# Three blocks on one core: first mixers regrouped, VectorE's head steps chained in TensorE's order, query's gate products moved behind the inverse's first level, odd mixer's end in steps

## The chip, the cores and the metric

The kernel runs on one NeuronCore of a Trainium2 chip. Its time is device microseconds of one launch. Three runs of the kernel before took 1113.0, 1119.35 and 1120.01 us (median 1119.35). A profiled execution of the same program gives the trace.

## The reference, cut to what matters

512 tokens of width 1024 in float32 go through three residual blocks.

```python
# block 1: two mixers beside each other, then a gated MLP
proj = rms_norm(x) @ w_in             # q k v gate a b of 4 delta heads, q k v gate of 4 retention heads
qkv  = silu(causal_dwconv(q, k, v))   # 4 taps
q, k = l2norm(q) * d**-0.5, l2norm(k)
beta, g = sigmoid(b), -exp(a_log) * softplus(a + dt_bias)
m    = strict_lower(k k^T * beta * decay(g));  t_mat = inv(eye + m)
# chunk by chunk: u = t_mat v' - w S;  o = q_dec S + (q k^T * decay) u;  S = S*cd + k_dec^T u
h    = x + concat(rms(o_gdn) * norm_w * silu(gate), rms(o_ret) * silu(gate)) @ w_out
h    = h + (silu(g) * u) @ w_down     # g, u: 3-tap convolutions of rms_norm(h) @ w_up
x    = rms_norm(h)
# block 2 (even mixer): window attention and multi-scale pooling, gated, @ ab_w_out
# block 3 (odd mixer)
a, b, gate = split(rms_norm(x) @ c_w_in)
conv = causal_dwconv(a * sigmoid(b), dw_w) + dw_b       # 31 taps, channel by channel
y    = silu(layer_norm(conv)) * silu(gate)
out  = x + rms_norm(y @ c_w_out)
```

## The kernel before, in words

Activations lie transposed: 8 tiles of 128 channels x 512 tokens. Every large matrix product is done in three passes (`mm3`, lines 320 to 323): operand and weight are each split into a rounded part "hi" (a ScalarE copy to fp32r) and a remainder "lo" (a subtraction on VectorE or GpSimd), and hi*hi, hi*lo and lo*hi are accumulated in PSUM. One unit of 128 output channels is 8 x 3 = 24 matmuls of 512 columns. Weights come through SyncE's DMA queue in a fixed order: `fetch` issues one, `unpack` splits it, `prefetch` does both while buffers are free, `take` hands the next one out. While `lazy` is set, `prefetch` only issues a load and splits it in its next call.

**Block 1's mixers** (lines 505 to 999). `side_steps` runs the projection units in the order of `P1_ORDER`; the first call does three units together and with them the 8 columns of a and b: per input tile k two narrow matmuls of the split input with the 16 columns `wab` (line 357). `first_norm` makes the rms factor `rbc`, `do_ab` then turns a and b into the decay exponents `g` and what hangs on them. The eight heads are Python generators (`gdn_head`, `ret_head`, `finish_head`) that give up control at each `yield from need(n, lat, cost)`: the main loop at line 988 resumes one when a clock, kept from estimated TensorE costs, has passed its `lat`, else it emits one more step of a projection unit. So TensorE's and SyncE's order is the traced order (`manual_schedule`, `P1_ENG`), head work mixed into projection work; ScalarE, VectorE and GpSimd are put in order by the framework's scheduler.
`gdn_head`: squares and their sums give the norms of q and k (line 667 sums q's squares with 4 matmuls of one column), `decays` and `decays_exp` make exp(g_i - g_j), then k k^T and k q^T (lines 695 to 698), the inverse by 32x32 tiles in four levels (`tiles`, line 723), two block steps and the scan over four chunks.

**Block 3** (lines 1325 to 1555). `P7_ORDER` is an order written by hand: a = two projection units and the gated product of tile m (`glu_tile`), t, u, v = a copy of the tile shifted four ways (`stack_tile`), c = the convolution (`conv_tile`), s = its statistics, g = a gate unit, x = transposes of the residual, l = `norm_stats`, b = `spread` of its two results, n = `norm_tile`. Of the 31 taps TensorE does 4 per group (`PE_TAPS` groups, line 1402), ScalarE and GpSimd 3 (`N_POOL`), VectorE the rest, two of them (`P7_LEAD`) into an SBUF tile and the others into the group's PSUM bank. Up to l, PE, SP and DVE are in traced order; from l on only PE and SP. The output product follows: tokens 0 to 255 first (lines 1594 to 1603), whose k-th step needs tile k of `Y` from `norm_tile` and the k-th weight.

Of the kernel before, what the change touches and what calls it, by code (L numbers as in the profile page):

```python
# [20 lines left out]
C = 128  # L21
# [15 lines left out]
L_A0 = 9.0  # L37
L_AB = 13.0
L_PRE = 4.6
L_NORM = 15  # L40
L_M = 5.2
# [23 lines left out]
PE_TAPS = (4, 4, 4, 4, 4, 4, 4, 4)  # L65
# [4 lines left out]
P7_ORDER = 'a0 a1 t0 g0 u0 a2 v1 c0 a3 v2 c1 s0 a4 v3 c2 s1 a5 v4 c3 s2 a6 v5 c4 s3 a7 v6 c5 s4 g1 v7 c6 s5 g2 c7 g3 s6 x0 g4 x1 s7 g5 x2 l0 g6 b0 n0 n1 n2 n3 n4 n5 g7 n6 n7 x3'  # L70
# [83 lines left out]
def build(tc, xT, par, cst, rope, w_ab, w_in, w_rv, w_out, w_up, w_down, a_w, ab_w, c_w, co_w, post1, poolw, out, dbg=None):  # L154
# [192 lines left out]
    def side_steps(ws, X, sl=slice(0, T), ab=None):  # L347


        ps = [pu() for _ in ws]  # L350
        if ab is not None:
            pab = pu()
        for k in range(KD):
            x = X[k][0][:, sl], X[k][1][:, sl]
            if ab is not None:
                for i in range(2):
                    pe.matmul(pab[0:16], lhsT=ab[:, 16 * k:16 * k + 16], rhs=x[i], start=k + i == 0, stop=k == KD - 1 and i == 1)
            for w, p in zip(ws, ps):
                mm3(p[:, sl], wsl(w, k), x, k == 0, k == KD - 1)
            if k % 4 == 3:  # L360
# [185 lines left out]
    fr(*xin)  # L546
# [6 lines left out]
    def first_norm():  # L553
        yield from need(1, L_N1)
        rstd.append(small(NCH, "rstd", 1))
        by_chunk(rstd[0], rsqrt_rows(rbc, ssum))

    Y, O, gate, G = [None] * 8, [None] * 8, [None] * 8, {}

    def do_ab(p):  # L560

        ab = al()
        TT(ab[0:16], p[0:16, :], rbc[0:16, :], MUL)
        yield from need(1, L_A0)
        pt = pm()
        for c in range(NCH):
            pe.transpose(pt[:, c * 16:(c + 1) * 16], ab[0:16, ch(c)], ident[0:16, 0:16])
        fr(ab)
        pt4 = pt[:, 0:64].rearrange("p (c e) -> p c e", c=4)
        pv = sp.tile([128, 4, 8], F32, name="pv", bufs=1)  # L570
        dve.tensor_copy(out=pv, in_=pt4[:, :, 0:8])
        TT(pv, pv, pt4[:, :, 8:16], ADD)
        pm.fr(pt)
        s = lambda n: sp.tile([128, 4, 4], F32, tag=n, name=n, bufs=1)
        xa, nx, ex, beta, ea, g = s("xa"), s("nx"), s("ex"), s("beta"), s("ea"), s("g")
        TT(xa, pv[:, :, 0:4], bc4(pc("dtb", 0, 4)), ADD)
        TS(nx, xa, -1.0, MUL)
        TT(nx, nx, xa, MAX)
# [3 lines left out]
        A(ea[:, 0, :], pc("alog", 0, 4), AF.Exp)  # L582
        STT(g, xa, -1.0, bc4(ea[:, 0, :]), MUL, MUL)
        A(beta, pv[:, :, 4:8], AF.Exp, scale=-1.0)
        TS(beta, beta, 1.0, ADD)
        dve.reciprocal(out=beta, in_=beta)
        g2 = g.rearrange("p c h -> p (c h)")
        yield from need(1, L_AB, 0.4)
# [19 lines left out]
    def decays_exp(gm):  # L608
# [11 lines left out]
    def gdn_pre(p, h, which):  # L620
# [4 lines left out]
        A(acc, acc, AF.Silu)  # L625
# [34 lines left out]
    def gdn_head(h, qT, kT, vT):  # L660
        gm, sq = decays(h), al()
        A(sq, qT, AF.Square)
        yield from need(3, L_PRE)
        Ec, Es = decays_exp(gm)
        pss = pm()
        for c in range(NCH):
            pe.matmul(pss[:, c:c + 1], lhsT=sq[:, ch(c)], rhs=ones[:, 0:1], start=True, stop=True)
# [26 lines left out]
        pkk, pkq = pm(), pm()  # L694
        for c in range(NCH):
            pe.matmul(pkk[:, ch(c)], lhsT=kT[:, ch(c)], rhs=kT[:, ch(c)], start=True, stop=True)
        for c in range(NCH):
            pe.matmul(pkq[:, ch(c)], lhsT=kT[:, ch(c)], rhs=qT[:, ch(c)], start=True, stop=True)
        for c in range(NCH):
            STT(Mt[:, ch(c)], pkk[:, ch(c)], f[:, c:c + 1], Es[:, ch(c)], MUL, MUL)  # L700
        for c in range(NCH):
            STT(At[:, ch(c)], pkq[:, ch(c)], f[:, c:c + 1], Ec[:, ch(c)], MUL, MUL)
        pm.fr(pk, pkk, pkq)
        fr(Ec, Es)
# [21 lines left out]
        cost = 2.2  # L726
# [977 lines left out]
```

## Time and profile before

| | us |
|---|---|
| runs | 1113.0, 1119.35, 1120.01 |
| profiled execution, its own time | 1112.05 |
| span of its instructions | 1110.1 |

The page gives busy time per engine, the granted TensorE clock and the chain of work that ended last; the trace answers questions on stretches, waits and single instructions. A matmul's busy time reaches past the start of the next one, since they are pipelined, so the cost of one is read here from start to start. A plain float32 product stands in the trace as two matmul records.

### The profile page before, as it was taken

What the parts mean: (1) busy time and instruction counts of PE and PEld (TensorE: products, weight loads), DVE (VectorE), ACT (ScalarE), POOL (GpSimd) and SP (SyncE); (2) the same over time, 40 slices, a digit from 0 to 9 for tenths busy, and PEclk for the clock granted to TensorE, in tenths of its full rate; (3) what the DMA queues carried; (4) which work ended last, traced back from release to release, by engine and by line L of the source; (5) the groups of instructions that cost most, each with busy time, mean ns of one, the idle gap of its engine ahead of it and who ended that gap; (6) DMA issues with size and microseconds to landing.
All of it is one profiled execution on the core that took longest, in us unless ns stands there. A gap on an engine that the chain in (4) does not pass through costs nothing.

```text
span 1110.1 us, 17768 instructions
## 1 busy us (share of the span) xinstructions
PE 1086.1 (98%) x6882; PEld 875.2 (79%) x6882; DVE 755.6 (68%) x1555; ACT 523.2 (47%) x1052; POOL 225.0 (20%) x208
## 2 busy tenths in 40 slices
PE   8989999999999999999999999999999999999997
PEld 5777787888888888888888888766899996666776
DVE  7969567577567876767653244679856858669774
ACT  6774353226444544444353255365445565454351
POOL 0562231101020000000000024000000016988350
PEclk9989999999999999999999999999999999999989
DMA  8331112113323323333333332211223322221112
GB/s 289 112 96 43 57 58 77 58 48 124 95 78 103 105 95 95 96 100 105 98 93 93 100 106 85 89 39 58 76 77 107 122 58 77 76 77 38 39 39 76
DMA packets 28948, 96.02 MB, mean 86 GB/s; under 512 B 3552, under 2 KB 3808, under 8 KB 28864
## 3 DMA queue, kind: packets, MB, share of 16 engines
q1 hardware_dynamic: 27936, 91.87, 26.0%
q0 software_dynamic: 928, 3.02, 0.9%
q8 instruction: 54, 0.88, 0.3%
q14 instruction: 30, 0.25, 0.1%
HBM read 92.78 MB, written 2.10 MB: 85 GB/s over the span
## 4 chain that ended last, share of the span: by engine, by line
PE 85%; DVE 8%; ACT 4%; DMA 1%; issue 1%; SPq 0%; DVEq 0%; ACTq 0%
PE bank L321 25%; PE bank L322 24%; PE bank L323 24%; PE bank L1402 3%; DVE act L169 2%; DVE act L172 1%; PE bank L1111 1%; ACT act L166 1%; PE bank L723 1%; ACT op L166 1%; PE bank L1149 1%; DVE stk L172 1%; PE bank L1386 1%; ACT whi L166 1%; ACT stk L166 1%
## 5 line engine op out<-in xcount | busy, mean ns | idle before, releaser
L321 PE MATMUL bank<-op,whi 128*128 128x512 f32 (+1 forms) x566 | 218.0, 385 | 1.4 <-DVE act L172 1.4
L321 PE MATMUL bank<-op,op 128*128 128x512 f32 (+1 forms) x547 | 212.5, 388 | 4.5 <-ACT op L166 3.5
L323 PE MATMUL bank<-op,wlo 128*128 128x512 f32 (+1 forms) x571 | 215.4, 377 | 0.0
L322 PE MATMUL bank<-op,whi 128*128 128x512 f32 (+1 forms) x570 | 213.9, 375 | 0.0
L322 PE MATMUL bank<-op,op 128*128 128x512 f32 (+1 forms) x543 | 206.0, 379 | 0.0
L323 PE MATMUL bank<-op,op 128*128 128x512 f32 (+1 forms) x542 | 204.3, 377 | 0.4 <-DVE op L169 0.4
L166 ACT ACTIVATE op<-raw 128x512 fp32r<-128x512 f32 (+1 forms) x168 | 103.6, 626 | 176.2 <-PE bank L322 159.8
L166 ACT ACTIVATE whi<-raw 128x512 fp32r<-128x512 f32 (+1 forms) x158 | 97.0, 623 | 160.9 <-PE bank L322 142.0
L321 PEld LDWEIGHTS bank<-op,op 128*128 128x128 f32 x547 | 103.4, 189 | 30.7 <-issue 5.0
L321 PEld LDWEIGHTS bank<-op,whi 128*128 128x128 f32 x566 | 107.9, 191 | 23.6 <-issue 3.7
L323 PEld LDWEIGHTS bank<-op,wlo 128*128 128x128 f32 x571 | 108.4, 190 | 19.9 <-issue 0.3
L322 PEld LDWEIGHTS bank<-op,whi 128*128 128x128 f32 x570 | 108.5, 190 | 18.8 <-issue 1.6
L323 PEld LDWEIGHTS bank<-op,op 128*128 128x128 f32 x542 | 102.7, 189 | 19.9 <-DVE op L169 0.8
L322 PEld LDWEIGHTS bank<-op,op 128*128 128x128 f32 x543 | 102.8, 189 | 18.4 <-issue 1.4
L169 DVE TENSOR_TENSOR op<-raw,op 128x512 fp32r<-128x512 f32 (+1 forms) x107 | 73.2, 693 | 46.0 <-ACT op L166 45.2
L169 POOL TENSOR_TENSOR act<-act,act 128x512 f32<-128x512 f32 x57 | 79.7, 1404 | 91.5 <-ACT act L166 84.7
L169 DVE TENSOR_TENSOR wlo<-raw,whi 128x512 fp32r<-128x512 f32 (+1 forms) x102 | 68.6, 678 | 29.6 <-ACT whi L166 29.4
L166 ACT ACTIVATE act<-act 128x512 f32<-128x512 f32 (+3 forms) x120 | 56.2, 476 | 46.4 <-DVE act L169 16.6
L322 PE MATMUL bank<-wlo,op 128*128 128x512 f32 (+1 forms) x203 | 72.0, 355 | 0.0
L169 DVE TENSOR_TENSOR bank<-bank,act 128x512 f32<-128x512 f32 x56 | 38.5, 694 | 48.7 <-PE bank L323 48.7
L321 PE MATMUL bank<-whi,op 128*128 128x512 f32 (+1 forms) x199 | 71.3, 358 | 0.0
L323 PE MATMUL bank<-whi,op 128*128 128x512 f32 (+1 forms) x195 | 70.5, 362 | 0.0
(382 smaller groups left out, 1749.0 us busy)
## 6 DMA issues: line engine op xcount, KB each, us to landing
raw<-in_w_up_dram SPq DMA_DIRECT2D x44, 512.0 KB, 3.5
raw<-in_w_in_dram SPq DMA_DIRECT2D x25, 512.0 KB, 3.6
raw<-in_c_w_dram SPq DMA_DIRECT2D x24, 512.0 KB, 3.7
raw<-in_a_w_dram SPq DMA_DIRECT2D x18, 512.0 KB, 3.5
raw<-in_w_down_dram SPq DMA_DIRECT2D x16, 448.0 KB, 3.3
raw<-in_w_out_dram SPq DMA_DIRECT2D x8, 512.0 KB, 3.5
raw<-in_w_down_dram SPq DMA_DIRECT2D x8, 512.0 KB, 3.5
raw<-in_ab_w_dram SPq DMA_DIRECT2D x8, 512.0 KB, 3.5
```

What stands on the lines that cost most here:

```text
L166: return act.activation(out=out, in_=in_, func=func, **k)
L169: return (e or dve).tensor_tensor(out=out, in0=in0, in1=in1, op=o)
L172: return (e or dve).scalar_tensor_tensor(out=out, in0=in0, scalar=scalar, in1=in1, op0=o0, op1=o1)
L321: pe.matmul(ps, lhsT=l[0], rhs=r[0], start=first, stop=False)
L322: pe.matmul(ps, lhsT=l[0], rhs=r[1], start=False, stop=False)
L323: pe.matmul(ps, lhsT=l[1], rhs=r[0], start=False, stop=last)
L723: pe.matmul(p[pt(i), c * c32:(c + 1) * c32], lhsT=l[pt(i), c * c32:(c + 1) * c32], rhs=r[pt(i), c * c32:(c + 1) * c32], start=True, stop=True)
L1111: pe.matmul(v2(psc[e])[:, i, lo:], lhsT=qT[sl, ch(b)], rhs=kT[sl, (b - 1) * C + lo:(b + 1) * C], start=True, stop=True)
L1149: pe.matmul(po[64 * e:64 * e + 64, ch(b)], lhsT=vtok[:, kb * C + 64 * e:kb * C + 64 * e + 64], rhs=v2(pT)[:, i, ch(j)], start=j == 0 or b ...
L1386: pe.matmul(pq[32 * j:32 * j + 32], lhsT=cc("eye")[sl], rhs=g[sl, LEFT + j:LEFT + j + T], start=True, stop=True)
L1402: pe.matmul(acc[32 * q:32 * q + 32], lhsT=wds[m][:, i * C + 32 * q:i * C + 32 * q + 32], rhs=st[:, o:o + T], start=i == 0, stop=i == n_e - 1)
```

## The change

In block 1: `wab` becomes 32 float32 columns per input tile (8 of them used, a and b's weight times the norm's weight) and the product with the unsplit input runs as two groups of four matmuls, each of the four in its own 32 columns of the array, after k = 3 and k = 7; `do_ab` sums the four and transposes them in one product with `eye`. `rsqrt_small` has 9 instructions in place of 12. `by_chunk`'s four copies go from VectorE to ScalarE. `do_ab` comes sooner (`L_A0` 9 to 5, `L_AB` 13 to 6), makes the decay products of three heads itself, and the Silu of the q, k, v tiles that are there by then is held back (`late`) until its last Exp. q's and k's squares are both summed by matmuls of 32 columns, and VectorE transposes the sums. k q^T and its four gate products move behind the first half level of the inverse. Each head step's VectorE instructions are put behind those of the step before (`turn`). The weight loads of this block are `lazy`, and a delayed split's instructions stand behind the last ScalarE instruction that `A` emitted.
In block 3: TensorE does 3 groups of taps on tiles 0 to 3, 4 on 4 to 6 and 6 on tile 7 (before 4 on each). `norm_stats` comes two gate units sooner (s7 and l0 ahead of g4 and g5), `norm_tile` is cut in three steps n, m, o, all on VectorE and ScalarE, with the last gate units between them. From l0 on VectorE and ScalarE are in traced order too, weight splits are lazy and wholly on ScalarE and VectorE, and the output weights are taken one by one.

```diff
-L_A0 = 9.0
-L_AB = 13.0
-L_PRE = 4.6
+L_A0 = 5.0
+L_AB = 6.0
+L_E = 1.8
+N_EARLY = 3
+L_PRE = 6.5
-L_M = 5.2
+L_M = 4.8
-PE_TAPS = (4, 4, 4, 4, 4, 4, 4, 4)
+PE_TAPS = (3, 3, 3, 3, 4, 4, 4, 6)
-... s5 g2 c7 g3 s6 x0 g4 x1 s7 g5 x2 l0 g6 b0 n0 n1 n2 n3 n4 n5 g7 n6 n7 x3'
+... s5 g2 c7 g3 s6 x0 s7 l0 g4 x1 b0 n0 n1 m0 n2 o0 m1 g5 x2 n3 o1 m2 n4 o2 m3 n5 o3 m4 g6 n6 o4 m5 o5 m6 g7 n7 o6 x3 m7 o7'
...
# prefetch
-            if ins is not None:
+            ins = ins or (landing and last[0])
+            if ins:
                 behind.enter_context(tc.issue_after(ins.ins))
...
# side_steps
-            if ab is not None:
-                for i in range(2):
-                    pe.matmul(pab[0:16], lhsT=ab[:, 16 * k:16 * k + 16], rhs=x[i], ...)
             for w, p in zip(ws, ps):
                 mm3(p[:, sl], wsl(w, k), x, k == 0, k == KD - 1)
+            if ab is not None and k % 4 == 3:
+                for j in range(4):
+                    o = 32 * (k - 3 + j)
+                    pe.matmul(pab[32 * j:32 * j + 32], lhsT=ab[:, o:o + 32], rhs=xin[k - 3 + j], ...)
...
# do_ab
+        A(ea[:, 0, :], pc("alog", 0, 4), AF.Exp)
+        TT(xa, pt4[:, :, 0:4], bc4(pc("dtb", 0, 4)), ADD)
+        TS(ge[:, 3], pt4[:, :, 4:8], -1.0, MUL)
+        STT(nx, xa, -1.0, xa, MUL, MAX)
         A(ex, nx, AF.Exp, scale=-1.0)
         A(ex, ex, AF.Ln, bias=1.0)
         STT(xa, xa, 0.0, ex, MAX, ADD)
         STT(g, xa, -1.0, bc4(ea[:, 0, :]), MUL, MUL)
+        gms = [decays(h) for h in range(N_EARLY)]
-        yield from need(1, L_AB, 0.4)
+        yield from need(2, L_AB, 1.3)
         pg = pm()
...
+        G["E", 0] = decays_exp(gms[0])
...
+        with tc.issue_after(G["last"].ins):
+            for x in late:
+                A(x, x, AF.Silu)
...
# gdn_head
-        for c in range(NCH):
-            pe.matmul(pss[:, c:c + 1], lhsT=sq[:, ch(c)], rhs=ones[:, 0:1], ...)
+        for a, t in enumerate(sq):
+            for b in range(4):
+                pe.matmul(v4(pss)[32 * b:32 * b + 32, a], lhsT=ones[:, 0:32], rhs=v4(t)[:, :, 32 * b:32 * b + 32], ...)
...
# step
+            if turn[0] is not None:
+                behind.enter_context(tc.issue_after(turn[0]))
...
# the odd mixer's end
             order.close()
-            order.enter_context(tc.manual_schedule(engines=P7_ENG))
+            order.enter_context(tc.manual_schedule(engines=P7_ENG | P7_ENG3))
+            lazy[0], lo_e[:] = True, (dve, dve)
             norm_stats()
...
     def norm_tile(m):
-        lbc = m0
         TT(cf[m], cf[m], rbc, MUL)
-        TT(cf[m], cf[m], lbc, ADD, e=gps if m % 2 else dve)
+        TT(cf[m], cf[m], m0, ADD)
         A(cf[m], cf[m], AF.Silu, scale=pc("lng", m), bias=pc("lnb", m))
+
+    def norm_gate(m):
         TT(cf[m], cf[m], gt[m], MUL)
-        Y.append(split(cf[m]))
-        fr(cf[m], gt[m])
+        fr(gt[m])
+        Y.append((alr(), alr()))
+        A(Y[m][0], cf[m])
+
+    def norm_rest(m):
+        TT(Y[m][1], cf[m], Y[m][0].bitcast(F32), SUB)
+        fr(cf[m])
```

## Rows read from the trace of the kernel before

**Rows 1.** The page's head and its row of busy time by engine.

```profile
span 1110.1 us, 17768 instructions
...
PE 1086.1 (98%) x6882; PEld 875.2 (79%) x6882; DVE 755.6 (68%) x1555; ACT 523.2 (47%) x1052; POOL 225.0 (20%) x208
```

**Rows 2.** Busy time by stretch: stretch and its length in us, then for PE, weight loads, DVE, ACT and POOL the busy us (instructions), then granted clock, DMA share and GB/s. The early heads, the later heads, the dense products up to block 3, and the start of the output product.

```profile
53.00:83.00 30.00, 26.05 (x132) 21.83 (x131) 21.52 (x63) 23.51 (x49) 21.13 (x18) 0.89 0.29 88
83.00:265.00 182.00, 179.42 (x2108) 148.31 (x2107) 127.44 (x385) 74.64 (x204) 34.52 (x47) 1.00 0.19 60
265.00:820.00 555.00, 554.72 (x2525) 447.17 (x2524) 360.11 (x672) 248.81 (x469) 34.78 (x35) 1.00 0.30 92
...
1051.50:1063.00 11.50, 6.97 (x18) 4.61 (x17) 11.50 (x12) 6.36 (x11) 7.15 (x5) 0.70 0.32 105
```

**Rows 3.** TensorE's waits: who waited for whom, us in total, times, longest us.

```profile
PE bank L667 <- ACT act L166: 1.8, 1, 1.8
PE bank L321 <- DVE act L172: 1.4, 1, 1.4
PE bank L795 <- DVE act L172: 1.0, 1, 1.0
PE bank L590 <- DVE g L172: 0.7, 1, 0.7
```

**Rows 4.** Busy time by stretch (columns as in rows 2): after the second head's wait, in the convolution, after the output product's wait.

```profile
66.00:73.00 7.00, 7.00 (x24) 5.92 (x24) 2.28 (x12) 5.85 (x20) 5.16 (x6) 0.52 0.34 116
940.00:960.00 20.00, 20.00 (x132) 13.69 (x132) 14.79 (x18) 8.76 (x15) 18.65 (x15) 1.00 0.20 69
1056.30:1063.00 6.70, 5.94 (x13) 4.25 (x14) 6.70 (x8) 3.84 (x8) 4.63 (x3) 0.50 0.27 80
```

**Rows 5.** Timeline of TensorE in the first projection: start us, us, engine, line, operation, out<-in, shape, count. Line 357 is the product for a and b, line 424 the sum of squares for the first norm.

```profile
12.17 0.63 PE L357 MATMUL bank<-op,whi 128*16 128x512 f32 x2
12.64 0.39 PE L321 MATMUL bank<-op,whi 128*128 128x512 f32 x1
...
14.71 0.63 PE L357 MATMUL bank<-op,whi 128*16 128x512 f32 x2
...
22.30 1.02 PE L424 MATMUL bank<-act,ck 128*128 128x512 f32 x2
```

**Rows 6.** Timeline of TensorE in the convolution: the sum of tile 0's result (line 1446), tile 7's four groups of taps (line 1402), and the first matmul of gate unit 4, which follows gate unit 3 and a set of residual transposes.

```profile
935.43 1.13 PE L1446 MATMUL bank<-act,ck 128*128 128x512 f32 x2
...
1015.40 3.64 PE L1402 MATMUL bank<-stk,act 128*32 128x512 f32 x32
...
1025.35 0.48 PE L321 MATMUL bank<-op,whi 128*128 128x512 f32 x1
```

**Rows 7.** Timeline of VectorE from the last sum of squares to the decay exponents g: that sum, `by_chunk`'s copies, the first copy of the transposed a and b, and g.

```profile
20.85 0.69 DVE L169 TENSOR_TENSOR act<-act,act 128x512 f32<-128x512 f32 x1
...
29.86 4.32 DVE L437 COPY rstd<-ry 32x4 f32<-32x4 f32 x4
...
43.89 0.18 DVE L571 COPY pv<-bank 128x32 f32<-128x32 f32 x1
...
53.56 1.13 DVE L172 SCALAR_TENSOR_TENSOR g<-xa,ea 128x16 f32<-128x16 f32 x1
```

**Rows 8.** Timeline of TensorE at the first two heads: sums of q's squares (line 667), transposes of k (line 657), and the second head's sums after their wait.

```profile
61.67 0.95 PE L667 MATMUL bank<-ck,act 128*128 128x1 f32 x8
62.48 0.63 PE L657 MATMUL bank<-ck,stk 128*128 128x128 f32 x4
...
65.77 1.43 PE L667 MATMUL bank<-ck,act 128*128 128x1 f32 x8 [1.76 <-ACT act L166]
```

**Rows 9.** Timeline of ScalarE before g: a table load and the Exp after it.

```profile
49.16 1.28 ACT L166 ACT_TABLE_LOAD   x1
50.45 0.22 ACT L166 ACTIVATE ex<-nx 128x16 f32<-128x16 f32 x1
```

**Rows 10.** Timeline of GpSimd: two decay products, and tile 6's statistics.

```profile
55.85 2.07 POOL L169 TENSOR_TENSOR act<-act,g 128x512 f32<-128x512 f32 x2
...
1018.66 6.07 POOL L169 TENSOR_TENSOR act<-act,act 128x512 f32<-128x512 f32 x4
```

**Rows 11.** Timeline of VectorE in block 3: tile 0's last two sums; the gated product and the accumulating taps of one tile with the idle time before them; tile 6's last tap; the first transpose of `norm_stats`; the first products of `norm_tile`.

```profile
929.74 1.48 DVE L169 TENSOR_TENSOR act<-act,act 128x512 f32<-128x512 f32 x2
...
979.12 0.69 DVE L169 TENSOR_TENSOR gp<-bank,act 128x512 f32<-128x512 f32 x1 [3.22 <-PE bank L323]
...
983.74 7.09 DVE L172 SCALAR_TENSOR_TENSOR bank<-gp,pr,bank 128x512 f32<-128x512 f32 x9 [1.58 <-PE bank L1402]
...
1017.16 0.75 DVE L172 SCALAR_TENSOR_TENSOR act<-gp,pr,bank 128x512 f32<-128x512 f32 x1
...
1039.17 0.72 DVE L430 STREAM_TRANSPOSE act<-bank 128x512 f32<-128x512 f32 x1 [7.14 <-PE bank L424]
...
1045.96 9.81 DVE L169 TENSOR_TENSOR act<-act,act 128x512 f32<-128x512 f32 x9
```

**Rows 12.** Timeline at the odd mixer's end: TensorE's last residual transposes, its first matmul of the output product, and ScalarE's first read of that product's first finished bank.

```profile
1050.76 1.04 PE L1497 MATMUL bank<-ck,act 128*128 128x128 f32 x8
...
1055.28 0.50 PE L321 MATMUL bank<-op,op 128*128 128x512 f32 x1 [3.49 <-ACT op L166]
...
1079.67 0.60 ACT L166 ACTIVATE act<-bank 128x512 f32<-128x512 f32 x1 [3.48 <-PE bank L323]
```

More of the change, by code (lines that the diff above doesn't have):

```diff
@@ L300, in take @@
     def take():
+        while not made:
+            prefetch()
         return made.popleft()
@@ L624, in gdn_pre @@
         conv_taps(acc, raw, [pc("gconv", j * 4 + 3 - s) for s in range(4)])
-        A(acc, acc, AF.Silu)
+        if late is None:
+            A(acc, acc, AF.Silu)
+        else:
+            late.append(acc)
         return acc
@@ L697, in gdn_head @@
         for c in range(NCH):
-            pe.matmul(pkq[:, ch(c)], lhsT=kT[:, ch(c)], rhs=qT[:, ch(c)], start=True, stop=True)
-        for c in range(NCH):
             STT(Mt[:, ch(c)], pkk[:, ch(c)], f[:, c:c + 1], Es[:, ch(c)], MUL, MUL)
[L701 to L704, printed above, removed]
+        pm.fr(pk, pkk)
+        fr(Es)
         c32, g4 = C // 4, range(4)
@@ L733, in gdn_head @@
             pm.fr(pz)
-            yield from need(1, L_Z, cost)
+            if n == 1:
+                pkq = pm()
+                for c in range(NCH):
+                    pe.matmul(pkq[:, ch(c)], lhsT=kT[:, ch(c)], rhs=qT[:, ch(c)], start=True, stop=True)
+                for c in range(NCH):
+                    STT(At[:, ch(c)], pkq[:, ch(c)], f[:, c:c + 1], Ec[:, ch(c)], MUL, MUL)
+                pm.fr(pkq)
+                fr(Ec)
+            yield from need(1, L_Z, 1.4 if n == 1 else cost)
             pb = pm()
@@ L894, in start @@
         wait.append((g, key, after))
+    turn = [None]
     def step(e):
-        try:
-            cost, lat = next(e[1])
-            clock[0] += cost
-            e[0] = clock[0] + lat
-        except StopIteration:
-            live.remove(e)
-            if e[2] is not None:
-                done.add(e[2])
+        n = len(tc.nc.cur_bb.bb.instructions)
+        with contextlib.ExitStack() as behind:
+            if turn[0] is not None:
+                behind.enter_context(tc.issue_after(turn[0]))
+            try:
+                cost, lat = next(e[1])
+                clock[0] += cost
+                e[0] = clock[0] + lat
+            except StopIteration:
+                live.remove(e)
+                if e[2] is not None:
+                    done.add(e[2])
+        for i in tc.nc.cur_bb.bb.instructions[n:]:
+            if i.engine == mybir.EngineType.DVE:
+                turn[0] = i
     def admit():
@@ L1546, in build @@
         nc.sync.dma_start(out=pst[j], in_=post1[:, j * T:(j + 1) * T])
-    ws = [take() for _ in range(KD)]
+    ws = []
     def p8_finish(c, ps, xt):
@@ L1596, in build @@
         for k in range(KD):
+            if len(ws) == k:
+                prefetch()
+                while not made:
+                    prefetch()
+                ws.append(take())
             for c in toks:
```

143 lines of the change are left out of this document (80 added, 63 removed).

## The prediction

> **What bounds the kernel now.** I read the page's head first: TensorE is busy 1086.1 of 1110.1 us [rows 1], so time can come only from TensorE work that is dropped and from its holes. Busy time is a weak witness (matmuls overlap in it), so I went on by stretch [rows 2]. From 265 to 820 us it lacks 0.3 of 555 us at clock 1.00, and the change touches nothing there. The holes lie where the change works: from 53 to 83 us TensorE is busy 26.05 of 30 us at a mean clock of 0.89; from 83 to 265 us it lacks 2.6 us; at the output product's start it is busy 6.97 of 11.5 us at 0.70. The list of waits names what ended them [rows 3]: ScalarE, VectorE twice, and g. [...]
>
> Prices. Nine wide matmuls lie between 12.64 and 14.71 us, 0.23 each [rows 5], so a unit of 24 takes 5.5. Four groups of taps take 3.64, 0.91 a group of four float32 products side by side in 32 columns each [rows 6].
>
> **The change, part by part.**
>
> *a and b.* Eight pairs of narrow matmuls at 0.47 (12.17 to 12.64) go: 3.8. Two groups of four float32 products in 32 columns come. The trace has this shape in the taps, 2 x 0.91 = 1.8 (bounds: nothing, and the old 3.8). Saved 1.9. But the first norm's sum on TensorE then comes at 20.4 in place of 22.3, and VectorE's last addition for it ends at 21.54 [rows 5, 7]: a wait of 1.1. Net -0.8 (-1.9 to 0). `do_ab`'s four transposes become four float32 products with 128 columns of weights, eight records as at line 667, 0.81 from 61.67 to 62.48 [rows 8]; less the old transposes +0.6 (0 to +0.8).
>
> *Norm sums.* Line 667's 0.81 goes from each of four heads. Eight products of 32 columns, 128 wide, come: two groups at a quarter of 0.91, 0.46, or as much as before if their 16 weight loads set the pace. -1.2 in all (-2.0 to 0). The square of all of k replaces four short ones on ScalarE; both are needed before the sums, and I cost that at nothing, since `L_PRE` (6.5 for 4.6) puts three more steps of projection ahead of it; without them it is one ScalarE pass, 0.6 as in [rows 12].
>
> *Early heads.* Lost here now: waits of 1.8 + 1.4 + 0.7 [rows 3] and half of 7.0 us at half clock [rows 4], 3.9 + 3.4 = 7.3. The wait at line 667 was ScalarE's backlog, with table loads in it. With the Silus held back, the copies off VectorE and `do_ab` early, this should go. What is late next is g itself. VectorE now ends `by_chunk` at 34.2 and reaches the transposed a and b at 43.89, 9.7 later [rows 7], behind three tiles' convolutions. Without the 4.32 of copies, three small instructions and the 0.8 above, this work starts at about 28.5 and a and b come up at 38.2. Then six short steps at 0.2 (xa, nx, Exp, Ln, xa, g) and 1.28 of table load [rows 9], and one tap (0.8) ahead of one of them: g at 41.5. TensorE ends the first projection at about 27.5 (28.3 before, from 22.3, the sum's 0.9 and two k of 2.1 + 0.47; less 0.8), needs 8 then 10 steps of three matmuls (0.69) and the 0.8 of products: it asks for g at 40.7. That is a wait of 0.8, and 1.0 more for GpSimd's first decay product [rows 10], behind which all projection units, SyncE's loads with them, stand in TensorE's queue. I add 1.2 as a third of one spell at half clock: +3.0. Net -4.3. Bounds: -7.3 if nothing is late; if from the first copy to g it takes as before (43.89 to 54.69, 10.8), g comes at 49.0, a wait of 8.3 with 1.0 and 3.4 behind it, net +5.4.
> [...]
>
> *Order of VectorE's head steps, gate products later.* The same instructions. Of the 2.6 that TensorE lacks from 83 to 265 us [rows 2], with a wait of 1.0 for VectorE as the longest named, I take half: -1.3 (-2.6 to 0, and the third rival).
>
> *Lazy loads, splits behind the last ScalarE instruction.* The same loads on SyncE, split one call later. The weights made ahead, several units of 5.5, cover it; without that cover each unit would wait for its own load. I cost it at nothing.
>
> *Taps.* 32 groups become 12 + 12 + 6 = 30: -1.8. VectorE gets four taps more on each of tiles 0 to 3, 7.09 / 9 = 0.79 each, 3.2 a tile, and was idle 3.22 + 1.58 = 4.8 in a tile [rows 11]; the tile is 0.9 shorter, so 0.7 stays free. Tile 0's result came at 931.2, TensorE asked for it at 935.43 [rows 6, 11]: 3.2 later against 1.8 earlier is a wait of 0.8. GpSimd is busy 18.65 of 20 us [rows 4] and gets no more. Net -1.0 (-1.8 to +1.4, if tiles 1 to 3 wait 0.8 too).
>
> *The end.* TensorE is done with the last transposes at 1051.8; 96 matmuls at 0.23 would end at 1073.9; ScalarE reads the first bank at 1079.67 [rows 12], so 5.7 are lost. The cause is in VectorE's row: nine products run back to back for 9.81 us before any tile is split [rows 11]. From the norm's sums (1039.2) to the output product TensorE has 12.6 us of other work now; afterwards four gate units and three sets of transposes, 25. The first tile of Y needs the norm's chain, 6.8 to 1045.96, four products at 0.7 and two ScalarE passes, about 11. Each further tile takes VectorE 2.8, and TensorE 12 x 0.23 = 2.8 for its k. The 14 us of lead also cover the weight splits that leave GpSimd, 16 x 0.7 = 11 at most. Is the norm's sum late, though, two gate units sooner? TensorE reaches it 6.3 after tile 7's taps (1019.04 to 1025.35) [rows 6]. Tile 7's two accumulating taps and two sums are done 3.0 after these taps. Tile 6's last tap now comes 8 after its own group and GpSimd ends its statistics 6.8 later (1017.9 to 1024.7) [rows 10, 11]; with 11 between the two groups that is 3.8 after tile 7's, and the last two additions end at 5.2. It is not late, by 1.1. s7 and l0 issue no loads; g4 and g5 issue theirs 1.9 later, still well ahead of the output product. -5.7 (to +0.7 if the sum comes 3 late and half clock follows).
>
> **Sum.** -0.8 + 0.6 - 1.2 - 4.3 - 1.3 - 1.0 - 5.7 = -13.7. The profiled execution took 1112.05, which gives 1098.4. The median of the runs is 7.3 above it; on that, 1105.6.
>
> **The rivals.**
> 1. *g is late.* The short time to g fails, since VectorE and ScalarE still serve three tiles first, as in the 10.8 of before. For it: the six steps cross from VectorE to ScalarE and back, each time behind what is queued there. Against: the queue is 4.3 shorter and the Silu tables are gone. The term is +5.4 in place of -4.3: 1115.3.
> 2. *The norm's sum is late.* The margin is 1.1, and GpSimd at 93% can use it up. 3 late and 3.4 of half clock put +0.7 in place of -5.7: 1112.0.
> 3. *The chain holds VectorE up (slower).* A head instruction that waits for its matmul now also holds every later head's instruction, and with them the projections' bank-emptying products; TensorE stopped 1.4 for such a bank already [rows 3]. There are 125 head steps. From 0.11 us of TensorE's time a step all is lost, from 0.20 it is over 1% slower; at 0.25, 31 us, 1136.9. Against: VectorE is busy 127 of 182 us there [rows 2], and the chained order is that in which TensorE makes the data.
>
> **How the numbers follow.** Forecast 0.60, its own range 1092 to 1109; rival 1 0.15; rival 2 0.15; rival 3 0.10. All best bounds together (-21.3) from the fastest run of 1113.0 give 1092, rivals 1 and 2 reach 1115: that is the range. A measurement of this kernel can tell about 1% from no change, 11.2 us. Faster by more: 0.57 of the forecast and 0.06 of a mild rival 2, 0.63; within 1%: 0.27; slower: 0.10.
>
> **What would show it.** Right: two groups for a and b at 0.9; no half clock between 60 and 75 us; a wait for g of 1 to 2; the output product's first matmul right behind the last transposes at full clock. Wrong: a wait of many us at the decay sums, a wait at the two row sums after tile 7, TensorE lacking clearly more than 2.6 us in the later heads, or growing waits at tiles 1 to 3.

## The result and the profile after

The changed kernel takes 1127.87 us (median of 6, 1124.35 to 1128.67), the kernel before beside it 1118.23 (1113.0 to 1120.28): ratio 1.0083 [1.0062, 1.0104]. The forecast was 1105.6, range 1092 to 1115. The change makes the kernel about 9 us slower.

The page of the changed kernel, head and busy row, against [rows 1]: the span is 16.5 longer, TensorE's work about the same.

```profile
span 1126.6 us, 17712 instructions
...
PE 1087.6 (97%) x6902; PEld 876.2 (78%) x6902; DVE 763.5 (68%) x1522; ACT 508.2 (45%) x1017; POOL 200.7 (18%) x194
```

Busy time by stretch of the changed kernel (columns as in [rows 2]): the stretches of [rows 2], two short ones inside the second, and the output product's start (its first matmul is at 1075.39).

```profile
53.00:83.00 30.00, 28.28 (x214) 22.66 (x214) 24.21 (x61) 14.80 (x28) 12.85 (x11) 1.00 0.25 73
83.00:265.00 182.00, 159.62 (x1896) 129.31 (x1895) 111.40 (x303) 56.84 (x147) 30.38 (x41) 0.92 0.15 47
265.00:820.00 555.00, 554.83 (x2567) 448.68 (x2566) 362.81 (x683) 250.14 (x487) 37.30 (x39) 1.00 0.30 93
...
83.00:93.00 10.00, 2.92 (x40) 2.07 (x39) 8.10 (x33) 3.00 (x7) 1.79 (x2) 0.81 0.12 48
161.00:172.00 11.00, 3.32 (x11) 2.47 (x10) 7.82 (x25) 3.12 (x5) 2.59 (x4) 0.65 0.16 49
...
1074.50:1086.00 11.50, 11.09 (x54) 8.90 (x53) 8.47 (x14) 8.12 (x15) 0.00 (x0) 1.00 0.24 73
```

The early heads gained, as was forecast: TensorE is busy 28.28 of 30 us at clock 1.00, where before it was 26.05 at 0.89. So did the end: at the output product's start TensorE is busy 11.09 of 11.5 us, where before it was 6.97. The loss lies in the second row: TensorE lacks 22.4 of 182 us there at clock 0.92, where before it lacked 2.6 at 1.00 [rows 2]. Two holes of 7 us stand out. TensorE's waits name who ended them:

```profile
PE bank L846 <- DVE stk L178: 7.7, 1, 7.7
PE bank L755 <- DVE act L175: 7.1, 1, 7.1
PE bank L330 <- ACT whi L171: 5.7, 1, 5.7
PE bank L755 <- DVE act L750: 3.5, 1, 3.5
PE bank L755 <- DVE act L780: 3.0, 2, 2.5
```

Line 755 is a half level of a head's inverse, line 846 a product of the scan; both wait for VectorE (the 5.7 for ScalarE is the start of the kernel). In the kernel before the scan's product (line 795 there) waited 1.0 [rows 3]. What VectorE did in the first hole is in its timeline (start, us, operation, out<-in, shape, count), and beside it TensorE's:

```profile
79.96 0.41 DVE L709 STREAM_TRANSPOSE act<-bank 128x256 f32<-128x256 f32 x1
80.29 1.30 DVE L175 TENSOR_TENSOR wlo<-raw,whi 128x512 fp32r<-128x512 f32 x1
...
82.18 0.15 DVE L182 TENSOR_SCALAR sse<-act 128x8 f32<-128x8 f32 x1
...
86.08 0.69 DVE L175 TENSOR_TENSOR stk<-bank,fl 128x512 f32<-128x512 f32 x1
86.68 0.68 DVE L175 TENSOR_TENSOR stk<-bank,rki 128x512 f32<-128x512 f32 x1
87.28 1.11 DVE L178 SCALAR_TENSOR_TENSOR act<-bank,f,act 128x128 f32<-128x128 f32 x4
89.76 0.29 DVE L175 TENSOR_TENSOR act<-act,act 128x128 f32<-128x128 f32 x1 [1.36 <-ACT act L171]
...
90.65 0.25 DVE L175 TENSOR_TENSOR act<-bank,act 128x128 f32<-128x128 f32 x1
```

```profile
77.77 0.64 PE L704 MATMUL bank<-act,ck 128*32 128x128 f32 x16
...
79.27 1.06 PE L732 MATMUL bank<-act 128*128 128x128 f32 x8
80.26 0.45 PE L755 MATMUL bank<-act 32*32 32x32 f32 x32
...
90.96 0.65 PE L755 MATMUL bank<-act 32*32 32x32 f32 x32 [7.08 <-DVE act L175]
```

TensorE makes the third head's norm sums (77.77), the second head's k k^T (79.27), then the first head's half level (80.26), and asks for its masked result 3.6 us later (90.96 less the wait of 7.08 is 83.88). That result is one VectorE instruction of 0.25 us, at 90.65. In front of it, in the chained order, stand the third head's norms (79.96 to 86.68, with a weight split and three taps in between that are not in the chain) and the second head's scalings and masks (86.68 to 90.6, of which VectorE itself waits 1.36 for ScalarE), which nobody awaits yet. After the hole TensorE's granted clock is 0.50 from 91 to 96 us and 0.87 in the mean from 93 to 118. The second hole is alike: a head's end and another head's norms fill VectorE from 157.7 to 169.06, then comes the 0.34 us for which line 846 has waited. Four small instructions in it take 0.58 to 1.19 us in place of 0.17; e8 and e11 below show why.

### The profile page after: what moved, and what is told of

It reads as the page before. It is cut to its first block, busy times and chain, and to the rows that moved or that the text cites. A ratio compares the mean times of both kernels' runs of the same rounds, so it can differ in the third digit from the quotient of the medians.

```text
span 1126.6 us, 17712 instructions
## 1 busy us (share of the span) xinstructions
PE 1087.6 (97%) x6902; PEld 876.2 (78%) x6902; DVE 763.5 (68%) x1522; ACT 508.2 (45%) x1017; POOL 200.7 (18%) x194
## 4 chain that ended last, share of the span: by engine, by line
PE 83%; DVE 10%; ACT 3%; issue 2%; DMA 2%; POOL 1%; SPq 0%; DVEq 0%; POOLq 0%; ACTq 0%
PE bank L330 24%; PE bank L331 23%; PE bank L332 23%; DVE act L175 2%; PE bank L1456 2%; DVE act L178 2%; PE bank L755 1%; PE bank L1162 1%; ACT act L171 1%; PE bank L1200 1%; DVE op L175 1%; DVE bank L178 1%; ACT op L171 1%; DVE wlo L175 1%; ACT whi L171 1%
## 5 line engine op out<-in xcount | busy, mean ns | idle before, releaser
L330 PE MATMUL bank<-op,whi 128*128 128x512 f32 (+1 forms) x575 | 224.0, 389 | 6.0 <-ACT whi L171 5.7
L331 PE MATMUL bank<-op,whi 128*128 128x512 f32 (+1 forms) x575 | 217.6, 378 | 0.0
L330 PE MATMUL bank<-op,op 128*128 128x512 f32 (+1 forms) x538 | 207.2, 385 | 0.4 <-ACT stk L171 0.4
L331 PE MATMUL bank<-op,op 128*128 128x512 f32 (+1 forms) x538 | 202.4, 376 | 0.0
L332 PE MATMUL bank<-op,op 128*128 128x512 f32 (+1 forms) x538 | 202.0, 375 | 0.0
L175 DVE TENSOR_TENSOR op<-raw,op 128x512 fp32r<-128x512 f32 (+1 forms) x140 | 97.2, 707 | 69.8 <-ACT op L171 69.4
L330 PEld LDWEIGHTS bank<-op,whi 128*128 128x128 f32 x575 | 109.2, 190 | 30.2 <-ACT whi L171 5.7
L331 PEld LDWEIGHTS bank<-op,whi 128*128 128x128 f32 x575 | 109.5, 190 | 20.0 <-issue 1.9
L330 PEld LDWEIGHTS bank<-op,op 128*128 128x128 f32 x538 | 101.4, 189 | 24.5 <-issue 3.4
L175 DVE TENSOR_TENSOR wlo<-raw,whi 128x512 fp32r<-128x512 f32 (+1 forms) x129 | 90.7, 709 | 41.1 <-ACT whi L171 40.7
L332 PEld LDWEIGHTS bank<-op,op 128*128 128x128 f32 x538 | 101.4, 188 | 18.6 <-issue 0.6
L331 PEld LDWEIGHTS bank<-op,op 128*128 128x128 f32 x538 | 101.6, 189 | 17.4 <-issue 1.3
L171 ACT ACTIVATE act<-act 128x512 f32<-128x512 f32 (+3 forms) x105 | 53.6, 519 | 78.3 <-DVE act L175 22.2
L330 PE MATMUL bank<-whi,op 128*128 128x512 f32 (+1 forms) x199 | 74.6, 375 | 0.0
L332 PE MATMUL bank<-whi,op 128*128 128x512 f32 (+1 forms) x199 | 73.2, 368 | 0.0
```

Of the source, the lines that this page charges most:

```text
L171: last[0] = act.activation(out=out, in_=in_, func=func, **k)
L175: return (e or dve).tensor_tensor(out=out, in0=in0, in1=in1, op=o)
L330: pe.matmul(ps, lhsT=l[0], rhs=r[0], start=first, stop=False)
L331: pe.matmul(ps, lhsT=l[0], rhs=r[1], start=False, stop=False)
L332: pe.matmul(ps, lhsT=l[1], rhs=r[0], start=False, stop=last)
```

## The experiments

Theory A: the chain costs the time. Theory B, the rival: the regrouped mixers themselves do (gate products moved, early decay work, delayed splits). Ratios are to the kernel before beside the same run.

| run | us | ratio [95%] |
|---|---|---|
| changed | 1127.9 | 1.0083 [1.0062, 1.0104] |
| e1 no chain | 1111.8 | 0.9931 [0.9916, 0.9945] |
| e2 chain alone | 1129.6 | 1.0093 [1.0072, 1.0115] |
| e3 block 3 alone | 1108.0 | 0.9907 [0.9887, 0.9926] |
| e4 mixers, no chain, old block 3 | 1119.3 | 1.0003 [0.9993, 1.0013] |
| e5 long steps out of the chain | 1111.2 | 0.9937 [0.9917, 0.9958] |
| e6 only long steps ahead | 1124.9 | 1.0063 [1.0042, 1.0083] |
| e7 e1, gate products in front | 1113.2 | 0.9953 [0.9937, 0.9969] |
| e8 e1, masks on VectorE | 1108.1 | 0.9905 [0.9878, 0.9931] |
| e9 e3, masks on VectorE | 1104.4 | 0.9873 [0.9852, 0.9894] |
| e10 e8, no splits on GpSimd | 1106.0 | 0.9898 [0.9872, 0.9923] |
| e12 e8, decay work late | 1113.8 | 0.9976 [0.9955, 0.9998] |
| f1 e8, splits at once | 1105.1 | 0.9889 [0.9859, 0.9918] |
| f2 e8, old norm sums | 1107.1 | 0.9905 [0.9876, 0.9933] |
| f3 e8, old lead times | 1109.7 | 0.9933 [0.9910, 0.9955] |
| f4 e9, no splits on GpSimd | 1106.5 | 0.9894 [0.9869, 0.9919] |
| g1 f1, no splits on GpSimd | 1101.1 | 0.9867 [0.9827, 0.9907] |
| g2 f1, old norm sums | 1100.5 | 0.9853 [0.9821, 0.9885] |

**e1: the chain out.**

```diff
-            if turn[0] is not None:
-                behind.enter_context(tc.issue_after(turn[0]))
```

> The changed kernel without the chain of VectorE's head steps; all else as changed. Theory A, that the chain costs the time (other heads' long VectorE steps are put ahead of the short ones that TensorE waits for): the four long waits for VectorE in the mixers (7.7, 7.1, 3.5 and 3.0 us) and the half clock behind them go, the mixers give back 20 to 25 us, and the time is 1103 to 1108. Theory B, that the regrouped mixers themselves are slower (the gate products behind the inverse's first level, the early decay work, the delayed splits): the waits stay in some form and the time is 1120 to 1128.

1111.8: 16.1 below the changed kernel. The chain costs the time, as theory A says; the time stays 4 above its range, so something else in the mixers costs too.

**e2: the chain in the kernel before.**

```diff
# before.step
+        with contextlib.ExitStack() as behind:
+            if turn[0] is not None:
+                behind.enter_context(tc.issue_after(turn[0]))
```

> The kernel before with the chain alone added. Theory A: waits of several us for VectorE appear at the inverse or the scan in the mixers, with half clock behind them, and the time is 10 to 25 us above the kernel before. Theory B: the time is within 4 us of the kernel before. If only the chain together with the regrouped mixers costs time, this run is near before and the run without the chain is fast too.

1129.6, 11.0 above before. The longest of TensorE's waits in it:

```profile
PE bank L795 <- DVE act L172: 7.2, 1, 7.2
```

The chain does it in either set of mixers, with the same hole at the scan (line 795 is there what 846 is in the changed kernel). Theory B is out as the cause of the loss.

**e3: block 3 alone.** The kernel before with the change's taps, order of the end, cut `norm_tile` and output weights.

```diff
-PE_TAPS = (4, 4, 4, 4, 4, 4, 4, 4)
+PE_TAPS = (3, 3, 3, 3, 4, 4, 4, 6)
...
-            order.enter_context(tc.manual_schedule(engines=P7_ENG))
+            order.enter_context(tc.manual_schedule(engines=P7_ENG | P7_ENG3))
```

> The kernel before with the changes to block 3 alone (taps per tile, the end in steps, output weights one by one), block 1 as before. Both theories: 6 to 9 us below before, of which the stall at the output product gives 5 to 6 and the taps 1 to 2. A result near before would say that the 8 us which the changed kernel gives back between the row sums ahead of block 3 and its end come from somewhere else.

1108.0, 10.6 below before (8.3 to 12.6 by the interval); more than the 6.7 forecast. From the fourth row sums, the last ahead of the odd mixer's, to the last instruction the trace has 327.7 us (778.2 to 1105.9), that of before 335.9 (774.2 to 1110.1): 8.2. With the changed mixers the same step is worth 7.5 (e4 less e1, below).

**e4: the regrouped mixers without the chain, block 3 of before.**

```diff
# e1 with
-PE_TAPS = (3, 3, 3, 3, 4, 4, 4, 6)
+PE_TAPS = (4, 4, 4, 4, 4, 4, 4, 4)
...
-            order.enter_context(tc.manual_schedule(engines=P7_ENG | P7_ENG3))
+            order.enter_context(tc.manual_schedule(engines=P7_ENG))
```

> The changed mixers of block 1 without the chain, block 3 as before. Theory A: the early stalls of before are gone and nothing takes their place, 4 to 8 us below before. Theory B: 5 to 20 us above before.

1119.3, no change against before. Neither theory's range: the early gain is there (28.87 busy of 30 from 53 to 83 us) and lost again from 83 to 265, where TensorE lacks 9.2.

**e5 and e6: which steps of the chain.** Long steps are the norms of q and k, the first scaling and masking, the heads' ends and the first norm, 8 to 17 VectorE instructions each, 17 of 143 steps (the prediction's 125 and the 18 of the heads' ends and the first norm); a head's end has a last step of one instruction, which goes with them.

```diff
# e5
+        long = e[1].__name__ in LONG or f.f_lineno in LONG
-            if turn[0] is not None:
+            if turn[0] is not None and not long:
...
-            if i.engine == mybir.EngineType.DVE:
+            if i.engine == mybir.EngineType.DVE and not long:
```

```diff
# e6: all steps wait, only long ones are waited for
-            if i.engine == mybir.EngineType.DVE:
+            if i.engine == mybir.EngineType.DVE and long:
```

> The changed kernel, its chain without the 17 long steps (norms of q and k, first scaling of v and k k^T, the heads' ends, the first norm: 8 to 17 VectorE instructions each); the short steps stay chained. Theory A1, the cost comes in lumps, where a long step of one head is put ahead of a short one of another: without them the time is within 5 us of the run without a chain (1111.8), so 1107 to 1117. Theory A2, the cost comes from every step, each wait for a matmul being passed on: most of the 16 us stay, 1122 to 1128.

> The complement: every step's VectorE instructions are put behind the latest long step, but not behind other short ones. Theory A1: the four long waits stay and the time is 1122 to 1129. Theory A2: 1110 to 1117.

e5 takes 1111.2, as without any chain, and e6 1124.9, which is 13.1 of the 16.1 that the chain costs. e6's waits show the two holes again:

```profile
PE bank L846 <- DVE stk L178: 8.1, 1, 8.1
PE bank L755 <- DVE act L175: 7.1, 1, 7.1
```

So the loss comes in lumps, where a long step is put ahead of another head's short one; the short steps chained among themselves cost nothing that can be measured, and gain nothing. The last 3.0 need both kinds in the chain.

**e7 and e8: two suspects in the mixers without the chain.**

```diff
# e7: k q^T and its four gate products beside k k^T again
# e8, decays_masked
-        TT(v4(Es), v4(Ec), bc4(cc("strict")), MUL, e=gps)
-        TT(v4(Ec), v4(Ec), bc4(cc("caus")), MUL, e=gps)
+        TT(v4(Es), v4(Ec), bc4(cc("strict")), MUL)
+        TT(v4(Ec), v4(Ec), bc4(cc("caus")), MUL)
```

> No chain, and the gate products of k q^T back beside k k^T as before (all else as changed). If moving them behind the inverse's first level is what takes back the early gain of the mixers: the stalls at the first head's inverse (1.9 and 1.0) go and the time is 1105 to 1109, below the 1111.8 of the run without a chain. If the move itself helps or does nothing: 1111 to 1116.

> No chain, and the two masks of each delta head's decays (128x512 products) on VectorE in place of GpSimd. Theory C, that a small VectorE instruction stands still while such a GpSimd instruction runs (three of 8 columns took 1.2 to 1.5 us in place of 0.15 beside three GpSimd instructions, ahead of the 3.7 us wait in the scan): two of the three go, that wait falls to about 1.5 and the time to 1107 to 1110. If the GpSimd instructions only happen to lie there: the wait stays near 3.7, and VectorE's eight products more (0.7 each) leave the time at 1112 to 1117.

e7 takes 1113.2: the move of the gate products (with the lead time and the bank counts that belong to it) is worth about 1.4, near the limit of what these runs tell apart, since e1's and e7's overlap. e8 takes 1108.1: the masks on GpSimd cost 3.7, and the wait of 3.7 at line 846 is gone from its list. What they do is seen in e1, ahead of its wait of 3.7 at line 846; VectorE, then GpSimd:

```profile
153.28 1.21 DVE L175 TENSOR_TENSOR rnt<-rn 128x8 f32<-128x8 f32 x1
...
154.55 0.15 DVE L175 TENSOR_TENSOR rnl<-rnt,sse 128x8 f32<-128x8 f32 x1
154.63 1.24 DVE L175 TENSOR_TENSOR orst<-or 128x4 f32<-128x4 f32 x1
...
155.87 1.48 DVE L178 SCALAR_TENSOR_TENSOR rnt<-rnl 128x8 f32<-128x8 f32 x1
```

```profile
153.19 1.28 POOL L175 TENSOR_TENSOR stk<-act,act 128x512 f32<-128x512 f32 x1
154.54 1.31 POOL L175 TENSOR_TENSOR act<-act,act 128x512 f32<-128x512 f32 x1
155.80 0.30 POOL L783 MEMSET act<- 64x256 f32 x1
156.07 1.25 POOL L175 TENSOR_TENSOR op<-raw,op 128x512 fp32r<-128x512 f32 x1
```

Three instructions of 4 or 8 columns (0.15 otherwise) end with the GpSimd product that they meet: 153.28 + 1.21 is 154.49, the mask ends at 154.47. The product for which line 846 waits stands behind them on VectorE.

**e9 to e12.**

```diff
# e9: e3 with e8's two lines
# e10: e8 with
-LO_B = (1, 0)
+LO_B = (0, 0)
# e11: e1, and behind its end stretches like
+            for _ in range(m):
+                TT(b2, b0, b1, MUL, e=gps)
+            for _ in range(n):
+                TS(s2, s0, 1.0, MUL)
# e12: e8 with
-L_A0 = 5.0
-L_AB = 6.0
+L_A0 = 9.0
+L_AB = 9.0
```

> The mixers of before with the masks of the decays on VectorE, and the changed block 3 (that is the run with block 3 alone, 1108.0, with the masks moved). If GpSimd's masks cost as much in the mixers of before (3.7 in the regrouped ones): 1103 to 1106. If they only hurt in the regrouped mixers, where two masks lie beside a head's end and the next head's norms: 1107 to 1110.

> No chain, masks on VectorE (1108.1), and from the tenth unit on also the weight splits on VectorE that GpSimd did (some 12 of 128x512). Theory C (a GpSimd instruction holds small VectorE ones up): little is left to win, one wait of 1 to 2, so 1105 to 1109. Theory D (VectorE itself is the limit of the heads): 12 products of 0.7 more on it lengthen the mixers, 1110 to 1118.

> The kernel without the chain, and behind its end a measurement of its own that the output doesn't use: VectorE instructions of five kinds, alone and beside five GpSimd products of 128x512 (and a sixth stretch beside memsets). Theory C: those with both operands in SBUF (8 columns, 0.15 alone) stand still until the GpSimd instruction has ended, about one for each 1.3 us; from PSUM they run on. If the GpSimd instruction only shares bandwidth: all of them are slower by some tens of per cent, none by 8 times.

> No chain, masks on VectorE (1108.1), the early decay work put back by 7 us of the order's clock (L_A0 9 for 5, L_AB 9 for 6). Theory D, that what the early heads gain up to 76 us is given back by 117 us because VectorE is then the limit: 1106 to 1111, no worse than early. If the early gain is kept: 1111 to 1116.

e9 takes 1104.4: the masks cost the old mixers as much, 3.7 (in e3 a projection unit at 82.83 us waits 3.3 behind a norm's small instructions, in e9 the one at 80.91 waits 1.5). e10 takes 1106.0, 2.1 below e8 with runs that overlap: not the loss of theory D. e12 takes 1113.8, 5.7 above e8: theory D, that VectorE gives back all of the early gain, falls. The measurement in e11 (one run of 1167.7, longer than e1 by its added work; only its trace is used), VectorE's stretches and then GpSimd's:

```profile
1099.37 6.96 DVE L175 TENSOR_TENSOR zc<-za,zb 128x8 f32<-128x8 f32 x10
...
1111.87 2.63 DVE L182 TENSOR_SCALAR zc<-za 128x8 f32<-128x8 f32 x13
...
1114.54 6.88 DVE L182 TENSOR_SCALAR zc<-za 128x8 f32<-128x8 f32 x10
...
1127.53 4.76 DVE L1690 COPY zc<-bank 128x8 f32<-128x8 f32 x24
...
1134.45 3.05 DVE L178 SCALAR_TENSOR_TENSOR act<-bank,za,act 128x128 f32<-128x128 f32 x8
...
1137.54 6.14 DVE L178 SCALAR_TENSOR_TENSOR act<-bank,za,act 128x128 f32<-128x128 f32 x16
...
1144.47 4.31 DVE L175 TENSOR_TENSOR act<-act 128x512 f32<-128x512 f32 x6
...
1148.82 9.76 DVE L175 TENSOR_TENSOR act<-act 128x512 f32<-128x512 f32 x7
...
1159.30 4.76 DVE L175 TENSOR_TENSOR zc<-za,zb 128x8 f32<-128x8 f32 x24
```

```profile
1099.55 6.75 POOL L175 TENSOR_TENSOR act<-act,act 128x512 f32<-128x512 f32 x5 [68.50 <-DVE zc L175]
...
1114.72 6.67 POOL L175 TENSOR_TENSOR act<-act,act 128x512 f32<-128x512 f32 x5 [8.41 <-DVE zc L182]
...
1149.01 8.30 POOL L175 TENSOR_TENSOR act<-act,act 128x512 f32<-128x512 f32 x5 [4.65 <-DVE act L175]
1159.44 4.60 POOL L1694 MEMSET act<- 128x512 f32 x8 [2.13 <-DVE act L175]
```

Alone, 13 small ones with one input take 2.63, 0.20 each; beside five GpSimd products 10 of them take 6.88, and 10 with two inputs 6.96: two for each product, of which, by e1's rows, one is held until the product ends. From PSUM copies of the same size run at 0.20 beside GpSimd (24 in 4.76) and the 128x128 gate products at 0.38 both ways. Beside memsets the two-input ones are not held (24 in 4.76). Theory C holds: held to the end, not slowed by a share.
e11 didn't try one-input instructions beside memsets, but the heads do. In the changed kernel's second hole one of 8 columns ends with the memset that it meets, VectorE, then GpSimd:

```profile
163.53 0.58 DVE L182 TENSOR_SCALAR rnt<-sse 128x8 int32<-128x8 int32 x1
...
163.55 0.53 POOL L747 MEMSET act<- 128x512 f32 x1 [1.71 <-DVE sse L182]
```

**f1 to f4: what takes back the early gain.**

```diff
# f1: e8 without
-    lazy[0] = True
     main = p1_units()
# f2: e8 with the squares and sums of q and k as before
# f3: e8 with
-L_PRE = 6.5
-L_M = 4.8
+L_PRE = 4.6
+L_M = 5.2
# f4: e9 with LO_B = (0, 0)
```

> No chain, masks on VectorE (1108.1), and the weights of block 1 split when their load is issued again, not one call later. The prediction put the delayed splits at nothing. If they are what takes back the early gain: 1101 to 1105. If they cost nothing: 1107 to 1110.

> No chain, masks on VectorE (1108.1), and the sums of squares of q and k in the way of before (four one-column products for q, ScalarE's own sums for k, no 128x256 transposition on VectorE). By the prediction the new sums save 1.2, so 1109 to 1111. If VectorE's transposition and the two full squares are what takes back the early gain: 1102 to 1106.

> No chain, masks on VectorE (1108.1), and the two lead times of the head order as before (L_PRE 4.6 for 6.5, L_M 5.2 for 4.8): the norm step comes sooner, the inverse later. If the order of the changed kernel asks for the inverse too soon after its inputs (waits of 1.9 and 1.9 at it): 1103 to 1106. If not: 1108 to 1112.

> The fastest kernel so far (mixers of before, masks on VectorE, changed block 3: 1104.4) with the weight splits off GpSimd from the tenth unit on. In the regrouped mixers that gave 2.1. Theory C: 1101 to 1104. Theory D (VectorE is the limit): 1104 to 1108.

f1 takes 1105.1, f2 1107.1, f3 1109.7, f4 1106.5. Splits at once gain 3.0, with runs that overlap; f2 fell between its two ranges; the new lead times are no worse than the old ones; f4 is 2.1 above e9 and in theory D's range, so in the old mixers the splits are better shared. Where the delayed splits cost shows at the first head's half levels, e8, then f1:

```profile
86.60 0.45 PE L755 MATMUL bank<-act 32*32 32x32 f32 x32 [1.89 <-DVE act L175]
90.56 0.45 PE L755 MATMUL bank<-act 32*32 32x32 f32 x32 [1.92 <-DVE act L750]
...
86.21 0.45 PE L755 MATMUL bank<-act 32*32 32x32 f32 x32 [0.52 <-DVE act L175]
89.17 0.45 PE L755 MATMUL bank<-act 32*32 32x32 f32 x32 [0.92 <-DVE act L750]
```

In e8 VectorE does a split of 1.34 at 80.95, ahead of the first of these results, and GpSimd one of 1.44 at 88.40, beside which a VectorE instruction of 4 columns ahead of the second takes 1.26. In f1 VectorE has no split from 76.97 to 89.52 and GpSimd none from 80.89 to 92.78. Behind them TensorE's clock is 0.87 from 93 to 103 us in e8 and 1.00 in f1.

**g1 and g2: do they add up.**

```diff
# g1: f1 with
-LO_B = (1, 0)
+LO_B = (0, 0)
# g2: f1 with f2's sums, in gdn_head
-        for a, t in enumerate(sq):
-            for b in range(4):
-                pe.matmul(v4(pss)[32 * b:32 * b + 32, a], lhsT=ones[:, 0:32], ...)
+        for c in range(NCH):
+            pe.matmul(pss[:, c:c + 1], lhsT=sq[:, ch(c)], rhs=ones[:, 0:1], ...)
```

> The regrouped mixers with the three things taken out that the runs found to cost time: no chain, masks on VectorE, weights split at once (1105.1), and also no splits on GpSimd from the tenth unit on. If the two smaller gains (3.0 and 2.1) add up: 1102 to 1104. If the splits at once had already filled VectorE: 1105 to 1108.

> No chain, masks on VectorE, weights split at once (1105.1), and the norm sums of before. If the new sums save the 1.2 of the prediction once the other costs are gone: 1106 to 1108. If they save nothing, as with the delayed splits: 1103 to 1106.

g1 takes 1101.1, g2 1100.5, the fastest of all, 1.5% under before. Both lie below every range expected of them.

| | new norm sums | old norm sums |
|---|---|---|
| splits delayed | 1108.1 (1106.4 to 1108.7) | 1107.1 (1105.8 to 1110.5) |
| splits at once | 1105.1 (1103.6 to 1107.5) | 1100.5 (1099.1 to 1101.4) |

With splits at once the old sums are 4.6 faster, and the runs of the two don't overlap; with delayed splits no difference shows. Part of the 4.6 is a wait of TensorE for ScalarE's squares at the second head's sums, the changed kernel, f1 and g2:

```profile
62.42 0.64 PE L704 MATMUL bank<-act,ck 128*32 128x128 f32 x16 [1.44 <-ACT act L171]
...
63.39 0.65 PE L704 MATMUL bank<-act,ck 128*32 128x128 f32 x16 [1.06 <-ACT act L171]
...
62.85 0.95 PE L702 MATMUL bank<-ck,act 128*128 128x1 f32 x8
```

In g2 TensorE is busy 29.32 of 30 us from 53 to 83:

```profile
53.00:83.00 30.00, 29.32 (x194) 25.02 (x193) 26.93 (x68) 18.21 (x53) 9.55 (x8) 1.00 0.22 70
83.00:265.00 182.00, 178.25 (x2053) 146.64 (x2052) 119.32 (x350) 72.12 (x197) 29.26 (x44) 1.00 0.20 63
```

## Why the prediction was wrong

| term | forecast | measured, by |
|---|---|---|
| order of VectorE's head steps | -1.3, with the next | +16.1 (changed - e1), +11.0 (e2) |
| gate products later | in the same | -1.4 (e1 - e7, runs overlap) |
| early heads | -4.3 | -5.7 (e8 - e12, 7 us of the order's clock; not the whole term) |
| norm sums | -1.2 | +1.0 (e8 - f2, within the noise), +4.6 (f1 - g2) |
| delayed splits | 0 | +3.0 (e8 - f1, runs overlap), +6.6 (f2 - g2) |
| taps and end | -6.7 | -10.6 (e3), -7.5 (e1 - e4), -8.2 in e3's trace |
| a and b | -0.2 | no run alone; a group takes 1.0 (0.9 forecast) |

**The step that failed** is "Order of VectorE's head steps, gate products later. The same instructions." I took the chain for a gain of 1.3, and its only cost for a wait for a matmul that is passed on, which I gave 0.10 as the third rival. That rival's mechanism, VectorE held up by order, came true, but its form was wrong: up to 0.25 us in each of 125 steps was priced, and e5 and e6 show that the short steps among themselves cost nothing and that the 17 long ones ahead of short ones cost 13 of the 16 us. Both reasons "against" were read wrongly. VectorE's 127 busy of 182 us [rows 2] is a mean over the stretch; from 83 to 93 us of the changed kernel, while TensorE stands for 7, it is busy 8.1 of 10, nearly all of it with work that nobody awaits yet. And that the chain follows the order in which TensorE makes the data is no comfort: TensorE makes a head's norm sums long before it asks for what comes of them (`L_NORM` 15), and a half level of the inverse just before (`L_Z` 1.8). Chained by when the data is made, the urgent instruction stands last.

**The mixers without the chain.** Their terms add up to a forecast of -7.0. Without the chain they gain nothing: e4 is level with before, and e1 is 3.8 above e3, which has the old mixers. The delayed splits and the new norm sums take the gain back; with both undone, g2 is 3.9 below e9, which has the old mixers and the same masks (the runs don't overlap, the intervals of the two ratios do).

**What held.** g came at 40.65 (41.5 forecast); TensorE's first product with it starts at 41.26 without a wait, the clock is 1.00 from 60 to 75 us, and rival 1 didn't come about. Two misses in this term went opposite ways, which is luck: the 3.0 forecast for a late g did not come, and of the wait of 1.8 at the second head's sums, which was to go, 1.4 stayed. Rival 2 didn't come about either: after tile 7 TensorE has no wait at the sums, and the output product follows its transposes at clock 1.00 (1074.50 to 1086.00), with one wait of 0.4. From the end of the transposes to the first bank read it takes 23.0 (1075.39 to 1098.41) in place of 27.9 [rows 12], 4.9 of the 5.7 forecast. The end and the taps together gave somewhat more than forecast (the table). A wait for tile 0's result was forecast at 0.8 and is 0.5.

**Two smaller steps that failed.** The norm sums were priced on TensorE: their 16 matmuls take 0.57 (0.46 forecast, 0.81 before). But VectorE got a 128x256 transposition (0.41), which is in no term, and ScalarE a second full square ahead of the sums, of which the prediction says "both are needed before the sums, and I cost that at nothing". That is the part that failed: at the second head it is a wait of 1.1 in f1 and none in g2. What makes up the rest of the 4.6 the runs don't show. And of the delayed splits, which are among the things that take the early gain back, it says "I cost it at nothing". It asked only whether the weights come in time, not where the splits' instructions fall; in e8 they fall ahead of the first head's half levels.

**The base.** The profiled execution of before had quick mixers: it reaches the row sums ahead of the MLP at 331.89 us, e3, whose block 1 has the same mixers, at 335.95 (the changed kernel at 355.31). Adding the 7.3 by which the median lies above that execution was right; the runs of before beside the changed kernel have their median 6.2 above it.

## What to carry to other kernels

Before an engine's instructions are put in a fixed order across independent chains, list for each when its result is asked for, not when its data is made: here some 10 us of other heads' long steps ahead of one instruction of 0.25 cost a wait of 7.1, with a clock of 0.50 from 91 to 96 us behind it. Leave long steps out of such a chain, to be placed freely; the short ones chained gained nothing here either.
A mean busy share says nothing on such a hole; look at the 10 us in which the work must be done. And work taken off the bounding engine must be priced on the engine that gets it: the sums that saved 0.24 us of TensorE a head made the kernel up to 4.6 slower.

## What the runs showed of the hardware

A small VectorE instruction with its operands in SBUF that meets a 128x512 product of GpSimd stands still to the product's end: 4 or 8 columns take 1.14 to 1.48 us in place of 0.15 to 0.17 (e1, 153.28 to 155.87; changed kernel, 159.10, 160.47 and 164.14), in e11 ten beside five products take 6.96, and three in a row made a 3.7 us wait (e1). Copies of 8 columns from PSUM (0.20 each) and gate products with one input from PSUM (0.38 each) aren't touched (e11). Beside a memset two-input ones aren't touched (24 in 4.76, e11); one with one input took 0.58 in place of 0.17, to the memset's end (changed kernel, at 163.53). Why it is so no run shows. Were long instructions held to the end too, two 128x512 products beside each other would take, by an estimate from e11's rows, 4.31 / 6 + 6.67 / 5 = 2.05 a pair; e11 shows 8.30 / 5 = 1.66, so they overlap in part, and how is not shown. The kernel had it all along: moving eight masks (5.5 us of VectorE's time) off GpSimd gained 3.7 in the mixers of before as well.
